# Background work of attention layer B split into steps that are issued a share apart, and weight scans reduced two loads later

## The chip, the cores and the metric

The kernel runs on one core of one Trainium2 chip. The metric is the time of one execution on the device in microseconds. One execution of each kernel is also profiled; its trace holds every instruction with start, duration and what released it.

The engines are called by the short names of the profile: PE is TensorE (matrix products and transposes; PEld is its weight load), DVE is VectorE, ACT is ScalarE, POOL is GpSimd, and SP is SyncE, which here issues the DMAs. SBUF is the on-chip memory that all engines read; PSUM is the memory into which PE writes its products.

## The reference

A two-layer encoder step over a prompt of 2048 rows and a sample of 64 rows, model width 1024. Each layer computes

```python
h = rms_norm(x, norm_g); q, k, v, gate = split(h @ w_in)
q, k = rms_norm per head(q) * q_g, rms_norm per head(k) * k_g     # heads of 64
s = q @ k.T * 64 ** -0.5 + bias          # bias depends on the distance only
p = softmax(s over a band of chunks of 64 rows)
x = x + ((p @ v) * silu(gate)) @ w_out
```

Layer A has 16 query heads on 2 key heads, a band of its own chunk and 2 before it, and a learned sink in the softmax. Layer B has 16 heads of its own for queries and keys, a band of its own chunk and 8 before it, and no sink. The sample attends to a cache of keys and values and to itself. Outputs are the two layers' result for prompt and sample and the newest keys and values of both layers.

## The kernel before

The program runs layer A, A's output projection, layer B, and B's output projection. The change bears on layer B. There the outer loop runs over 8 **head pairs** (two heads, 128 columns each of q, k, v and gate), the next one over **units** of 256 rows (8 of the prompt, then the sample), each of two **tiles** of 128 rows.

For each tile the input projection makes 512 columns in PSUM (`pj`, lines 673 to 680; the operands are split into high and low 16-bit parts, hence three products a step). `evacuate_b` copies q and k to `pa` (L714, ACT), the high part of v to `values` (L718, ACT), the low part of v (L719, DVE, which reads L718's result), and the gate to `pb` (L722, ACT). `head_norm` squares q and k (L755, POOL), sums per head (L756, DVE), adds epsilon and takes the power -1/2 (L759, L760, POOL), and scales q and k in place (L773, DVE). `gate` takes a tanh (L781, ACT) and multiplies (L782, DVE). PE transposes q and k (L843); ACT copies the high parts (L1357, L1358) and DVE subtracts for the low parts (L1369, L1373); small DMAs (L1362) copy query rows from one half of the partitions to the other.

The attention of a unit has four steps, one for each head and tile (`scores`): PE writes scores to one of **two** PSUM buffers named `sb` (L1418, L1419); DVE adds the bias and takes the row maximum (L1422, which writes `p` to SBUF and the maximum to `nm`, and so frees `sb`); DVE adds a constant to `nm` (L1427); ACT takes the exponential with its row sum (L1431); ACT and POOL split `p` in two 16-bit parts (L1465, L1466), which a transposing DMA turns (L1474). Some steps later PE multiplies with the values into the PSUM buffer `o` (L1563 and others; two halves for the high and the low part). After the fourth step DVE takes the inverse of the row sums (L1439), POOL multiplies it with the gate (L1450, tile `G`), PE transposes `G` into an `sb` buffer (L843), and ACT copies that to `gt` (L1237). `finish_pairs` adds the two halves of `o` (copy L1247 on ACT, sum L1249 on DVE, after which `o` is free), multiplies with `gt` (L1250, POOL), and the result is stored (L1252, SP). The sample has its own outputs (L1521, L1525 to L1528).

Layer B's weights are used in 16-bit parts, scaled by their largest entry. `scan` loads pieces of the next head pair's weights (and of the output weights and the cache) and DVE reduces each to its maximum (L174); `input_across`, `everywhere` make scales of them.

What sets the order: PE runs in the order in which the program is written. The other engines' instructions are put in order by the framework's scheduler, which simulates all engines; waits between engines are semaphores. Each engine then runs its list strictly in that order, so an instruction that waits holds up all that follow it. Evacuated tiles leave their remaining work in the queue `bg` (class `Background`): `put(cost, fn, urgent)` adds an item, and `share(least, parts, few)`, called after each attention step, runs items up to a cost of `max(1.8, cost / 4)`. What an item issues is tied behind the last softmax instruction of its engine (`anchor`). A `Filler` issues projection matmuls between the attention steps, so that PE has work, and `due` runs what an earlier step has left for a later one (`LAG = 4` steps for the turned products).

Of the kernel before, what the change touches and what calls it, by code (L numbers as in the profile page):

```python
# [34 lines left out]
WB = 3  # L35
# [15 lines left out]
LAG = 4  # L51
HALF = 5 * 2 * P
# [3 lines left out]
def hybrid_encoder_kernel(  # L56
# [114 lines left out]
    def scan(i=None):  # L171
        if pending:
            j, raw = pending.pop()
            nc.vector.tensor_reduce(  # L174
                most[:, j : j + 1], raw, axis=AX.X, op=ALU.max, apply_absolute_value=True
            )
# [15 lines left out]

    def across(a, b):
        ps = psum("tp", 512, 1)
# [14 lines left out]
    def everywhere(h, o):  # L209
        ps = psum("tp", 512, 1)  # L210
        nc.tensor.matmul(ps[:, 0:3], ones[0:1, 0:1].to_broadcast([1, P]), o, start=True, stop=True)
        nc.vector.tensor_copy(scl[:, h], ps[:, 0:3])
# [14 lines left out]
    def input_scales(h):  # L227
        everywhere(h, row[:, 20:23])
        nc.vector.tensor_scalar(gsb[:, h], gain[:, 1, :], S_W(h), 1.0, op0=ALU.mult, op1=ALU.mult)
# [25 lines left out]
    def scale_work(hp, u, e):  # L255
        at = 2 * u + e
        if hp < 7:
            if at < 8:
                scan(8 * (hp + 1) + at)
            elif at == 8:  # L260
                scan()
# [6 lines left out]
            if 11 <= at < 14 and i < 84:  # L268
                scan(i)
            elif at == 14:  # L270
                scan()
# [15 lines left out]
    def bias_vectors_a():  # L287
        oh = held["oh"]
        ps = psum("tp", 512, 1)
# [79 lines left out]
    class Background:  # L369
        def __init__(self):  # L370
            self.queue, self.anchors, self.cost, self.lazy = [], {}, 0.0, False

        def put(self, cost, fn, urgent=False, lazy=False, weights=False):
            it = Item()
            it.fn, it.cost, it.urgent, it.weights = fn, cost, urgent, weights
# [41 lines left out]
        def share(self, least, parts, few):  # L417
            left = sum(it.weights for it in self.queue)
            self.drain(max(least, self.cost / parts), 1 if left <= few else 2)

    bg = Background()

    def load_weights(g, *specs, scale=None):
        dt = F32R if scale is None else F16
# [80 lines left out]
    def load_act(  # L505
        src, o, T, squares=False, joint=False, lead=None, cache=None, cached=False, dt=F32R,
        rows=None, scale=None,
    ):
        x = Item()
# [123 lines left out]
    def token_rows(unit):  # L633
        _, T, tiles = unit
        ps = psum("tp", 512, 1)
# [75 lines left out]
    def evacuate_b(hp, tt, ps, g):  # L711
# [7 lines left out]
        nc.vector.scalar_tensor_tensor(  # L719
            vh[:, :, HD:P], v, c, vh[:, :, 0:HD], op0=ALU.mult, op1=ALU.subtract  # L720
        )
# [24 lines left out]
    def head_norm(n, src, spread=True):  # L746
# [3 lines left out]
        def squares():  # L750
            sq = t("sq", [P, 256], 2)
            f.append(t("f", [P, 4], 3))
            fv = f[0][:n, :H]
            if spread:
                nc.gpsimd.tensor_tensor(sq[:n, : H * HD], src, src, op=ALU.mult)  # L755
                nc.vector.tensor_reduce(  # L756
                    fv, sq[:n, : H * HD].rearrange("p (h d) -> p h d", d=HD), axis=AX.X, op=ALU.add
                )
                nc.gpsimd.tensor_tensor(fv, fv, small[:n, :H], op=ALU.add)  # L759
                nc.gpsimd.tensor_tensor(fv, fv, mhalf[:n, :H], op=ALU.pow)  # L760
# [8 lines left out]

        def scale():  # L770
# [4 lines left out]
        return [bg.put(0.15 * H, squares, True), bg.put(0.1 * H, scale, True)]  # L775

    def gate(n, g):
        def fn():
            W = g.shape[1]
            e = t("sq", [P, 256], 2)  # L780
            nc.scalar.activation(e[:n, :W], g, AF.Tanh, scale=0.5)  # L781
            nc.vector.scalar_tensor_tensor(g, e[:n, :W], 1.0, g, op0=ALU.add, op1=ALU.mult)  # L782

        return [bg.put(0.3, fn)]
# [6 lines left out]
    def store_kv(layer, rows, kn, v, kdst, vdst):  # L791
# [9 lines left out]
        return bg.put(0.1, fn)  # L801
# [64 lines left out]
    class Filler:  # L866
# [9 lines left out]
        def step(self):  # L876
            if self.gen is None:
# [22 lines left out]
            if not self.attending:  # L900
                bg.drain(FR * c)
# [9 lines left out]
    def layer_a():  # L911
# [4 lines left out]
        def add_unit(qd, place, unit):  # L916
# [59 lines left out]
            def first():  # L976
# [7 lines left out]
                for i, c in enumerate(both([project(it.tile, xc, st.w[qd], 512, o) for it, o in zip(mine, qgs)])):  # L984
                    if i == 7:
                        token_scales(unit, xc, psum("tp", 512, 1))
# [75 lines left out]
        def turned(it, done):  # L1062
            tp = psum("tp", 512, 1)
# [169 lines left out]
    def gate_t(GT, n, scale=0.5):  # L1233
        J = GT.shape[1]
# [7 lines left out]
    def finish_pairs(Ov, gtv, n, dst, later=False):  # L1242
# [5 lines left out]
        for hh, rows in enumerate(halves):  # L1248
            nc.vector.tensor_tensor(o1v[rows], Ov[0:64, :, hh, :], o1v[rows], op=ALU.add)  # L1249
        nc.gpsimd.tensor_tensor(o1v, gtv, o1v, op=ALU.mult)  # L1250
        if later:
            held["later"].append(lambda: store(dst, o1v))  # L1252
        else:
            store(dst, o1v)

    def layer_b():
# [4 lines left out]
        def add_unit(hp, unit):  # L1261
# [23 lines left out]
            def gen():  # L1285
# [9 lines left out]
                for e, (tt, t0, n) in enumerate(tiles):  # L1295
                    out = []
                    c = yield from project((tt, t0, n), xc, st.w[hp], 512, out)
                    if last:
# [3 lines left out]
                        it.todo += [sums] + head_norm(P, pr[:, 0:128]) + gate(P, it.gate[:, e, 0:HD])  # L1302
                        it.todo.append(
                            store_kv(1, slice(n, P), kn, v, kb_s[192:256, cols], vb_s[192:256, cols])
# [7 lines left out]
                    it.todo += head_norm(n, pr[:n, 0:256]) + gate(n, it.gate[:n, e])  # L1312
                    if it is its[0] and e == 0:
                        block_scales(TOK - OT)
                    if tt >= NT - 4:
                        o = (tt - (NT - 4)) * P
                        it.todo.append(
                            store_kv(1, slice(0, P), kn, v, kb_p[o : o + P, cols], vb_p[o : o + P, cols])
# [13 lines left out]
        def queries(it):  # L1332
# [8 lines left out]
            tp = psum("tp", 512, 1)  # L1341
# [43 lines left out]
        def scores(it, i, h):  # L1385
# [52 lines left out]
            if c == w - 1:  # L1438
                nc.vector.reciprocal(it.sm[:n, :w], it.sm[:n, :w])  # L1439
                if turned(it, 0) and len(TURNED) == 1:  # L1440
                    part = it.sm[:n, TURNED[0] : w : 2]
                    nc.vector.tensor_scalar(part, part, PB, 1.0, op0=ALU.mult, op1=ALU.mult)
                it.G = G = t("G", [P, 256])
                if u == NU:
                    nc.gpsimd.tensor_tensor(
                        G[:, 0:HD], it.gate[:, 0, 0:HD], it.sm[:, 0:1].to_broadcast([P, HD]), op=ALU.mult
                    )
                    return
                for e in range(len(tiles)):
                    nc.gpsimd.tensor_tensor(  # L1450
                        G[:n, e * P : (e + 1) * P].rearrange("p (h d) -> p h d", d=HD),
                        it.gate[:n, e].rearrange("p (h d) -> p h d", d=HD),
                        it.sm[:n, 2 * e : 2 * e + 2].unsqueeze(2).to_broadcast([n, 2, HD]),
                        op=ALU.mult,
                    )
# [60 lines left out]

        def sample_outputs(it):
            O = psum("o", 512, 1)
# [11 lines left out]
        def sample_turned(it):  # L1530
            tp = psum("o", 512, 1)
# [7 lines left out]
        def turned_products(it, h):  # L1539
# [3 lines left out]
            if h == 0:  # L1543
                it.O = psum("o", 512, 1)
# [26 lines left out]
        def gates(it):  # L1571
            u, T, tiles = it.unit
            n = tiles[0][2]
            GT = psum_b("sb", 1024, 2) if it.hp and len(TURNED) else psum("tp", 512, 1)
# [4 lines left out]
        def finish(it):  # L1579
# [6 lines left out]
                True,  # L1586
            )
            finished[1, u] = finished.get((1, u), 0) + 1

        def products(it, h):  # L1590
# [13 lines left out]
            def begin():  # L1604
                if h == 0:
                    it.O = psum("o", 512, 1)
# [23 lines left out]
        def pipeline():  # L1630
# [63 lines left out]
            while todo:  # L1694
                filler.to(filler.done + 2.6)
                due(step)
                step += 1
            flush()
# [228 lines left out]
```

## Time and profile before

| | |
|---|---|
| time, median of 3 runs (lowest to highest) | 2230.35 us (2230.12 to 2232.27) |
| the profiled execution's own time | 2230.04 us |
| its span in the profile | 2228.3 us |
| instructions | 40988 |
| mean granted clock of PE | 0.979 |
| busy: PE | 2078.6 us (93%) |
| busy: DVE | 1520.2 us (68%) |
| busy: ACT | 1436.8 us (64%) |
| busy: POOL | 1140.4 us (51%) |
| chain that ended last | PE 45%, DVE 21%, ACT 9%, DMA 9%, issue 8%, POOL 6% |
| layer A | about 0 to 650 us |
| A's output projection | to about 870 us |
| layer B | about 870 to 2050 us |
| B's output projection | to the end |

A row of a timeline gives start, duration, engine, line, operation, output and input by the program's names, shapes, and in brackets the engine's idle time before it with what released it. A row of the waits gives an engine's instruction, what it waited for, the time in total, how often, and the longest. Line numbers are those of the kernel before.

### The profile page before, as it was taken

The numbers are of one execution on the slowest core, as the hardware profiler recorded it, in microseconds if no ns is written. First come the engines' busy times: TensorE is split into PE (matmuls) and PEld (weight loads), VectorE is DVE, ScalarE is ACT, GpSimd is POOL, SyncE is SP. The second block draws the span as 40 slices with busy tenths as digits, with TensorE's granted clock in tenths as the row PEclk, the third lists the DMA queues.
The fourth block names the chain that finished last, engine by engine and source line by source line (L and its number), as shares of the span: only waits on it lengthen the run. The fifth ranks groups of instructions, "written<-read, shape, count | busy, mean of one in ns | idle before, by whom it ended". The sixth has DMA issues, their size and how long they took to land.

```text
span 2228.3 us, 40988 instructions
## 1 busy us (share of the span) xinstructions
PE 2078.6 (93%) x12951; PEld 1477.0 (66%) x12951; DVE 1520.2 (68%) x4049; ACT 1436.8 (64%) x3610; POOL 1140.4 (51%) x1621
## 2 busy tenths in 40 slices
PE   7999999999999999999988988899898898898999
PEld 6887888787889997555554544455455454456788
DVE  6769778677676456878676676766867767568542
ACT  6888778677784333666666666766766667567430
POOL 5645644343454456763565665656656566465100
PEclk9999999999999999999999999999999999999999
DMA  8856547756546667544677686886867858568764
GB/s 274 281 158 215 170 138 216 229 164 186 165 128 198 207 204 233 180 158 139 155 186 181 151 223 139 180 204 138 200 172 175 212 139 183 137 135 187 209 199 124
DMA packets 512122, 404.97 MB, mean 182 GB/s; under 512 B 303697, under 2 KB 449377, under 8 KB 511873
## 3 DMA queue, kind: packets, MB, share of 16 engines
q1 hardware_dynamic: 511904, 402.35, 66.3%
q8 instruction: 102, 1.67, 0.3%
q14 instruction: 116, 0.94, 0.1%
HBM read 257.59 MB, written 73.43 MB: 149 GB/s over the span
## 4 chain that ended last, share of the span: by engine, by line
PE 45%; DVE 21%; ACT 9%; DMA 9%; issue 8%; POOL 6%; SPq 1%; ACTq 0%; POOLq 0%; DVEq 0%
PE pj L678 7%; PE pj L680 7%; PE pj L679 7%; PE pj L1770 4%; PE pj L1772 4%; PE pj L1771 4%; DVE p L1422 4%; DVE pa L773 3%; DMA scan<-in_w_in_b_dram 3%; PE sa L843 2%; POOL values L1466 2%; DVE q L1369 2%; DVE o L1249 2%; ACT p L1431 2%; DMA scan<-in_w_o_b_dram 1%
## 5 line engine op out<-in xcount | busy, mean ns | idle before, releaser
L678 PE MATMUL pj<-wh,xx 128*128 128x512 f16 (+2 forms) x1648 | 649.1, 394 | 4.0 <-ACT pb L701 1.7
L680 PE MATMUL pj<-wh,xx 128*128 128x512 f16 (+2 forms) x1648 | 630.7, 383 | 2.4 <-POOL xx L563 2.4
L679 PE MATMUL pj<-wh,xx 128*128 128x512 f16 x1024 | 396.7, 387 | 0.9 <-DVE wh L469 0.9
L1431 ACT ACTIVATE p<-p,nm 128x640 f32<-128x640 f32 (+5 forms) x264 | 198.8, 753 | 250.6 <-DVE nm L1427 210.1
L1466 POOL TENSOR_TENSOR values<-p,values 128x640 f16<-128x640 f32 (+2 forms) x224 | 281.5, 1257 | 133.7 <-ACT values L1465 131.2
L1770 PE MATMUL pj<-xx,wh 128*128 128x264 f32 (+1 forms) x1024 | 291.2, 284 | 7.1 <-DVE res L1776 3.6
L1771 PE MATMUL pj<-xx,wh 128*128 128x264 f32 (+1 forms) x1024 | 288.6, 282 | 0.0
L679 PE MATMUL pj<-wl,xx 128*128 128x512 f32 (+1 forms) x624 | 234.3, 375 | 2.3 <-DVE wl L469 2.3
L563 POOL TENSOR_TENSOR xx<-xraw,xx 128x528 fp32r<-128x528 f32 (+4 forms) x144 | 184.0, 1296 | 88.9 <-ACT xx L562 82.4
L1422 DVE CUSTOM_DVE_ANT_0 p<-sb,BT 128x640 f32<-128x640 f32 (+5 forms) x272 | 195.9, 720 | 30.2 <-PE sb L1419 26.8
L760 POOL TENSOR_TENSOR f<-f,mhalf 128x4 f32<-128x4 f32 (+2 forms) x187 | 186.9, 999 | 13.4
L680 PEld LDWEIGHTS <-xx 128*128 128x128 f16 x1024 | 102.0, 100 | 130.3 <-issue 11.1
L1250 POOL TENSOR_TENSOR o<-gt,o 128x256 f32<-128x256 f32 (+1 forms) x132 | 102.4, 776 | 159.1 <-ACT p L1156 89.9
L773 DVE TENSOR_TENSOR pa<-pa,f 128x256 f32<-128x256 f32 (+3 forms) x221 | 150.4, 681 | 46.8 <-POOL f L760 42.2
L755 POOL TENSOR_TENSOR sq<-pa 128x256 f32<-128x256 f32 (+2 forms) x187 | 115.5, 618 | 107.6 <-ACT pa L714 66.3
L1156 ACT ACTIVATE p<-p,nm 128x257 f32<-128x257 f32 (+2 forms) x272 | 134.3, 497 | 48.7 <-DVE nm L1150 42.0
L678 PEld LDWEIGHTS <-xx 128*128 128x128 f16 x1024 | 102.2, 100 | 84.5 <-issue 6.3
L679 PEld LDWEIGHTS <-xx 128*128 128x128 f16 x1024 | 102.0, 100 | 83.8 <-issue 9.5
L1465 ACT CAST values<-p 128x640 f16<-128x640 f32 (+2 forms) x224 | 147.1, 657 | 5.8
L1772 PE MATMUL pj<-xx,wl 128*128 128x264 f32 x512 | 145.7, 285 | 0.3 <-DVE wl L462 0.3
L1772 PE MATMUL pj<-xx,wh 128*128 128x264 f16 x512 | 142.1, 277 | 0.0
L1150 DVE CUSTOM_DVE_ANT_0 p<-sa,BT,nsink 128x256 f32<-128x256 f32 (+2 forms) x272 | 117.4, 468 | 36.1 <-PE sa L843 31.4
(272 smaller groups left out, 5029.3 us busy)
## 6 DMA issues: line engine op xcount, KB each, us to landing
xx<-xsb SPq DMA_DIRECT2D x112, 512.0 KB, 4.2
xx<-xsa SPq DMA_DIRECT2D x88, 512.0 KB, 4.8
xraw<-oga SPq DMA_DIRECT2D x64, 264.0 KB, 3.5
xraw<-ogb SPq DMA_DIRECT2D x64, 264.0 KB, 3.9
xsa<-xx SPq DMA_DIRECT2D x32, 512.0 KB, 4.1
scan<-in_w_in_b_dram SPq DMA_DIRECT2D x64, 256.0 KB, 4.7
wl<-in_w_in_b_dram SPq DMA_DIRECT2D x64, 256.0 KB, 5.4
xraw<-in_x_dram SPq DMA_DIRECT2D x40, 256.0 KB, 4.0
```

Source lines behind the costliest of these rows:

```text
L563: nc.gpsimd.tensor_tensor(lo, rv, wide(hi), op=ALU.subtract)
L678: nc.tensor.matmul(ps[:n, :C], xh, wh, start=k == 0, stop=False)
L679: nc.tensor.matmul(ps[:n, :C], xh, wl, start=False, stop=False)
L680: nc.tensor.matmul(ps[:n, :C], xl, wh, start=False, stop=k == KC - 1)
L760: nc.gpsimd.tensor_tensor(fv, fv, mhalf[:n, :H], op=ALU.pow)
L773: nc.vector.tensor_tensor(sv, sv, fv.unsqueeze(2).to_broadcast([n, H, HD]), op=ALU.mult)
L1422: mi = nc.vector.tensor_tensor_reduce(out=p[r, :nk], in0=S[r, o : o + nk], in1=b, op0=ALU.add, op1=ALU.min, scale=1.0, scalar=3e38, accum_ ...
L1431: ex = nc.scalar.activation(p[:n, :nk], p[:n, :nk], AF.Exp, scale=-1.0, bias=it.nm[:n, c : c + 1], accum_out=it.sm[:n, c : c + 1],)
L1466: lo = nc.gpsimd.tensor_tensor(two[:, :, 1, :], pv, two[:, :, 0, :], op=ALU.subtract)
L1770: nc.tensor.matmul(ps[:, :OT], wh, oh, start=k == 0, stop=False)
L1771: nc.tensor.matmul(ps[:, :OT], wh, ol, start=False, stop=False)
L1772: nc.tensor.matmul(ps[:, :OT], wl, oh, start=False, stop=k == KC - 1)
```

## The change

Five things, all in the way that work is handed to `bg`.

- `evacuate_b`: the low part of v (L719) is an item of its own. `head_norm` in layer B (`apart=True`) becomes three items, squares, sums and scale, and `gate` two, tanh and product. An item can name one that must run before it (`after`), and `drain` skips it in the share in which that one ran (`tick`).
- `finish_pairs`: the sum L1249, the product L1250 and the store are an item that is put as urgent; the ACT copies L1247 are issued at once.
- `scores`: the inverse sums (L1439) and gate products (L1450) of a unit become an item, run at the latest by `gates`.
- `everywhere`: the copy of the scales (and the scaled gains) become an item.
- `scan`: a load is reduced when the next one but one has been issued (`keep=1`, three buffers `wraw` in place of two buffers `scan`).

Buffers: `sq` 4 in place of 2, `f` 4 in place of 3. Whatever reuses a PSUM buffer or needs a result runs the items that are left first (`run_all`, `tp_bank`, `o_bank`).

```diff
     def scan(i=None, keep=0):
-        if pending:
-            j, raw = pending.pop()
+        while len(pending) > keep:
+            j, raw = pending.pop(0)
...
-            raw = t("scan", [P, 512], 2)
+            raw = t("wraw", [P, 512], WB) if keep else t("scan", [P, 512], 1)
...
+    def run_all(name):
+        while held[name]:
+            bg.run(held[name].pop(0))
...
         def run(self, it):
+            if it.after is not None:
+                self.run(it.after)
+            it.tick = self.tick
...
         def drain(self, budget, most=KC):
+                if it.after is not None and (it.after.fn is not None or it.after.tick == self.tick):
+                    continue
...
-        nc.vector.scalar_tensor_tensor(
-            vh[:, :, HD:P], v, c, vh[:, :, 0:HD], op0=ALU.mult, op1=ALU.subtract
-        )
+        def low():
+            nc.vector.scalar_tensor_tensor(
+                vh[:, :, HD:P], v, c, vh[:, :, 0:HD], op0=ALU.mult, op1=ALU.subtract
+            )
+        held["rest"].append(bg.put(0.2, low, True))
...
-        return [bg.put(0.15 * H, squares, True), bg.put(0.1 * H, scale, True)]
+        first = bg.put(0.15 * H - 0.1 * apart, squares, True)
+        if not apart:
+            return [first, bg.put(0.1 * H, scale, True)]
+        second = bg.put(0.1 * H, sums, True, after=first)
+        return [first, second, bg.put(0.1 * H, scale, True, after=second)]
...
-        return [bg.put(0.3, fn)]
+        if not apart:
+            return [bg.put(0.3, curve)]
+        first = bg.put(0.2, curve)
+        return [first, bg.put(0.2, product, after=first)]
...
+        def fn():
+            for hh, rows in enumerate(halves):
+                nc.vector.tensor_tensor(o1v[rows], Ov[0:64, :, hh, :], o1v[rows], op=ALU.add)
+            nc.gpsimd.tensor_tensor(o1v, gtv, o1v, op=ALU.mult)
+            if key:
+                held["later"].append(last)
...
+        if key:
+            held["ends"].append(bg.put(0.8, fn, True))
...
             if c == w - 1:
-                nc.vector.reciprocal(it.sm[:n, :w], it.sm[:n, :w])
+                item = bg.put(0.8, fn, True)
+                if u != NU:
+                    it.inverse = item
...
+        def o_bank():
+            run_all("rest")
+            run_all("ends")
+            return psum("o", 512, 1)
```

Below is what the change makes of VectorE's list at three places of one head pair, before and after. In the rows, L1422 is the softmax (its second row reads out the row maximum), L1427 the addition to `nm`; the numbers behind the names tell the buffers apart. In the changed kernel the same instructions have other line numbers: L1422 is L1491, L1427 is L1496, L773 is L811, L782 is L831, L1439 is L1519, L719 is L749, L756 is L802, L1249 is L1306.

VectorE at the end of a unit, the norm scale of `pa_3538` and the unit's last softmax; before:

```order
L773 TENSOR_TENSOR pa_3538_18044<-pa_3538_18044,f_3545_18073 128x256
L1422 ISA p_3552_18108,nm_3527_17969<-sb_3551_18107,BT_95 128x640
L1422 ISA nm_3527_17969 128x1
L782 SCALAR_TENSOR_TENSOR pb_3514_17884<-sq_3550_18097,pb_3514_17884 128x128
L1427 TENSOR_SCALAR nm_3527_17969<-nm_3527_17969 128x1
L1439 RECIPROCAL sm_3526_17968<-sm_3526_17968 128x4
```

and changed:

```order
L1491 ISA p_3552_18106,nm_3527_17965<-sb_3551_18105,BT_95 128x640
L1491 ISA nm_3527_17965 128x1
L811 TENSOR_TENSOR pa_3538_18044<-pa_3538_18044,f_3545_18073 128x256
L831 SCALAR_TENSOR_TENSOR pb_3514_17882<-sq_3550_18096,pb_3514_17882 128x128
L1496 TENSOR_SCALAR nm_3527_17965<-nm_3527_17965 128x1
L1519 RECIPROCAL sm_3526_17964<-sm_3526_17964 128x4
```

The softmax stands ahead of the norm scale; the addition to `nm` and the inverse sums stay behind both.

VectorE in the next unit, around the second softmax (`p_3571` before, `p_3570` changed); before:

```order
L719 SCALAR_TENSOR_TENSOR values_2360_11645<-pj_3549_18086,values_2360_11645 128x2x64
L1427 TENSOR_SCALAR nm_3562_18172<-nm_3562_18172 128x1
L756 TENSOR_REDUCE f_3566_18185<-sq_3565_18184 128x4
L1422 ISA p_3571_18211,nm_3562_18172<-sb_3570_18210,BT_95 128x640
L1422 ISA nm_3562_18172 128x1
L773 TENSOR_TENSOR pa_3558_18159<-pa_3558_18159,f_3566_18185 128x256
L782 SCALAR_TENSOR_TENSOR pb_3548_18085<-sq_3567_18191,pb_3548_18085 128x128
L1427 TENSOR_SCALAR nm_3562_18172<-nm_3562_18172 128x1
L1422 ISA p_3577_18256,nm_3562_18172<-sb_3576_18255,BT_95 128x640
```

and changed:

```order
L749 SCALAR_TENSOR_TENSOR values_2360_11645<-pj_3549_18084,values_2360_11645 128x2x64
L1496 TENSOR_SCALAR nm_3562_18165<-nm_3562_18165 128x1
L802 TENSOR_REDUCE f_3566_18182<-sq_3565_18181 128x4
L225 TENSOR_SCALAR gsb_91<-gain_77,scl_90 128x8
L1491 ISA p_3570_18205,nm_3562_18165<-sb_3569_18204,BT_95 128x640
L1491 ISA nm_3562_18165 128x1
L1496 TENSOR_SCALAR nm_3562_18165<-nm_3562_18165 128x1
L811 TENSOR_TENSOR pa_3558_18156<-pa_3558_18156,f_3566_18182 128x256
L831 SCALAR_TENSOR_TENSOR pb_3548_18083<-sq_3567_18186,pb_3548_18083 128x128
```

The addition to `nm` that belongs to this softmax has moved from behind the norm scale and the gate product to directly behind the softmax.

VectorE where that unit ends, around the sum of `o` (`o1_3600` before, `o1_3599` changed); before:

```order
L1439 RECIPROCAL sm_3561_18171<-sm_3561_18171 128x4
L782 SCALAR_TENSOR_TENSOR pb_3548_18085<-sq_3582_18293,pb_3548_18085 128x128
L1249 TENSOR_TENSOR o1_3600_18363<-o_3572_18227,o1_3600_18363 64x256 x2
L773 TENSOR_TENSOR pa_3578_18276<-pa_3578_18276,f_3581_18287 128x256
L1422 ISA p_3605_18378,nm_3603_18376<-sb_3604_18377,BT_95 128x640
L1422 ISA nm_3603_18376 128x1
L469 SCALAR_TENSOR_TENSOR wh_3594_18330<-wl_3586_18303,gsb_91,wh_3594_18330 128x512
L1427 TENSOR_SCALAR nm_3603_18376<-nm_3603_18376 128x1
```

and changed:

```order
L831 SCALAR_TENSOR_TENSOR pb_3548_18083<-sq_3582_18288,pb_3548_18083 128x128
L1519 RECIPROCAL sm_3561_18164<-sm_3561_18164 128x4
L811 TENSOR_TENSOR pa_3578_18273<-pa_3578_18273,f_3581_18286 128x256
L1491 ISA p_3604_18370,nm_3602_18368<-sb_3603_18369,BT_95 128x640
L1491 ISA nm_3602_18368 128x1
L1306 TENSOR_TENSOR o1_3599_18358<-o_3572_18224,o1_3599_18358 64x256 x2
L496 SCALAR_TENSOR_TENSOR wh_3593_18326<-wl_3585_18295,gsb_91,wh_3593_18326 128x512
L1496 TENSOR_SCALAR nm_3602_18368<-nm_3602_18368 128x1
```

The sum of the two halves of `o` has moved from ahead of the norm scale and the next unit's first softmax to behind both.

PE's list is the same in both kernels, instruction by instruction, and so are all lists up to the end of layer A's output projection. ACT's L722 no longer carries a wait for DVE and stands directly behind L718.

More of the change, by code (lines that the diff above doesn't have):

```diff
@@ L51 @@
 LAG = 4
+SQB = 4
 HALF = 5 * 2 * P
@@ L421, in hybrid_encoder_kernel @@
     bg = Background()
+    held["rest"], held["ends"], held["scales"] = [], [], []
     def load_weights(g, *specs, scale=None):
+        run_all("scales")
         dt = F32R if scale is None else F16
@@ L1247, in finish_pairs, with fn, last @@
             nc.scalar.copy(o1v[rows], Ov[64:128, :, hh, :])
[L1248 to L1252, printed above, removed]
+        def fn():
+            for hh, rows in enumerate(halves):
[3 more added lines that the diff above has]
+                held["later"].append(last)
+            else:
+                store(dst, o1v)
+        def last():
+            store(dst, o1v)
+            finished[key] = finished.get(key, 0) + 1
+        if key:
+            held["ends"].append(bg.put(0.8, fn, True))
         else:
-            store(dst, o1v)
+            fn()
     def layer_b():
@@ L1697, in pipeline @@
                 step += 1
+            run_all("ends")
             flush()
```

147 lines of the change are left out of this document (91 added, 56 removed).

## The prediction

> **What bounds the kernel now.** I read the stages first (the windows view; after the stretch and its length come the busy time of PE, PEld, DVE, ACT and POOL with their instructions, PE's granted clock, the DMA share and GB/s), because the diff touches only what surrounds layer B.
>
> ```profile
> 870.00:2050.00 1180.00, 1065.50 (x6229) 609.38 (x6230) 835.34 (x2165) 790.19 (x1957) 706.96 (x948) 0.97 0.70 172
> ```
>
> PE is the bound: it works 1065.5 of layer B's 1180 us, and no other engine passes 71%. What can be had is PE's idle 114.5 us and a little clock. The work is the same before and after, and PE's own order is the same instruction by instruction, so the time changes only by how long PE stands. Next came what PE waited for in this stretch (engine and line, what it waited for, us in total, times, longest).
>
> ```profile
> PE sb L1418 <- DVE nm L1422: 46.9, 26, 3.9
> PE sb L1418 <- DMA q<-q: 12.7, 5, 4.3
> ...
> PE sb L843 <- DVE nm L1422: 5.4, 5, 1.7
> PE sb L1418 <- ACT gt L1237: 4.2, 7, 0.7
> ```
>
> The scores (L1418) have two PSUM buffers, and the softmax on VectorE (L1422) frees them: 46.9 us are PE waiting for VectorE to get to it. The same waits list over all engines tells why VectorE is late: it runs its list in order, and often the head of that list is itself waiting.
>
> ```profile
> ACT pb L722 <- DVE values L719: 64.1, 66, 2.4
> ...
> DVE o L1249 <- ACT o L1247: 39.3, 42, 1.4
> DVE pa L773 <- POOL f L760: 37.4, 40, 2.0
> ...
> DVE most L174 <- DMA scan<-in_w_in_b_dram: 30.2, 15, 4.6
> ```
>
> Last came PE's timeline. Layer B repeats per head pair; the gaps of one repetition are these (start, us, line, then in brackets the idle time before it and its releaser; two rows without a bracket are used further down).
>
> ```profile
> 1389.66 0.32 PE L1418 MATMUL sb<-KA,q 128*128 128x384 f16 x1 [2.24 <-DVE nm L1422]
> ...
> 1392.97 0.32 PE L1418 MATMUL sb<-KA,q 128*128 128x384 f16 x1
> ...
> 1407.18 0.32 PE L1418 MATMUL sb<-KA,q 128*128 128x384 f16 x1 [1.49 <-DVE nm L1422]
> ...
> 1410.49 0.32 PE L1418 MATMUL sb<-KA,q 128*128 128x384 f16 x1 [0.66 <-ACT gt L1237]
> ...
> 1422.60 0.32 PE L1418 MATMUL sb<-KA,q 128*128 128x384 f16 x1 [1.64 <-DVE nm L1422]
> ...
> 1427.78 1.26 PE L1563 MATMUL o<-pt,values 128*128 128x256 f16 x12
> ...
> 1437.92 0.41 PE L843 MATMUL sb<-ident,G 128*128 128x128 f32 x2 [0.94 <-DVE nm L1422]
> ...
> 1441.64 0.32 PE L1418 MATMUL sb<-KA,q 128*128 128x384 f16 x1 [2.66 <-DVE nm L1422]
> ...
> 1468.31 0.32 PE L1418 MATMUL sb<-KA,q 128*128 128x384 f16 x1 [2.25 <-DMA q<-q]
> ...
> 1486.24 0.36 PE L1521 MATMUL o<-VS,ph 128*128 128x256 f32 x1 [1.06 <-ACT p L1431]
> ```
>
> I call them A (1389.66), B (1407.18), C (1410.49), D (1422.60), E (1437.92), F (1441.64), Q (1468.31) and S (1486.24). Four of them, A, B, D and F, are L1418 waiting for L1422, and that wait occurs 26 times: 26 / 4 = 6.5 repetitions. So I price one repetition and multiply by 6.5.
>
> **Part by part.**
>
> *Norm scale behind the softmax (A, B, C).* In the changed order L1422 stands ahead of the norm scale L773. Here are the rows around A, with a second L773 for comparison.
>
> ```profile
> 1387.13 1.61 DVE L773 TENSOR_TENSOR pa<-pa,f 128x256 f32<-128x256 f32 x1
> 1388.77 0.82 DVE L1422 CUSTOM_DVE_ANT_0 p<-sb,BT 128x640 f32<-128x640 f32 x1
> ...
> 1389.72 0.15 DVE L1427 TENSOR_SCALAR nm<-nm 128x1 f32<-128x1 f32 x1
> ```
>
> ```profile
> 1387.07 1.39 POOL L1466 TENSOR_TENSOR values<-p,values 128x640 f16<-128x640 f32 x1 [0.55 <-ACT values L1465]
> ```
>
> ```profile
> 1426.03 0.43 DVE L773 TENSOR_TENSOR pa<-pa,f 128x256 f32<-128x256 f32 x1
> ```
>
> ```profile
> 1392.44 0.47 ACT L1237 ACTIVATE gt<-sb,scl 128x256 f32<-128x256 f32 x1
> ```
>
> Swapped, L1422 starts at 1387.13 instead of 1388.77, so A's direct part is 1.6 of 2.24, and B, with the same swap, loses all its 1.49. But A is followed by a score at 1392.97 that starts just as the gate copy L1237 ends (1392.44 + 0.47 = 1392.91): that hangs on the last exponential, which waits for L1427, and L1427 still stands behind both. So PE, early at A, stands at the gate copy instead; after B the same happens at C, which grows. What stays is by how much the pair gets shorter. L773 takes 1.61 where it starts beside L1466 on POOL and 0.43 otherwise; it ends at 1388.74, 0.28 after L1466 (1387.07 + 1.39 = 1388.46). Begun 0.82 later, it would still end at about 1388.75, with L1422 already done: L1427 0.77 earlier. Bounds for A, B and C together: 0 if L773 always takes 1.61, and 2.24 + 1.49 = 3.73 if C does not grow. I take 2 x 0.77 = **-1.5**, the value of the rows next to it. [...] By a fixed 1.61 this term would be 0.
>
> *Softmax log sum ahead of norm and gate (D).*
>
> ```profile
> 1414.85 1.40 DVE L782 SCALAR_TENSOR_TENSOR pb<-sq,pb 128x128 f32<-128x128 f32 x1
> 1416.17 0.14 DVE L1427 TENSOR_SCALAR nm<-nm 128x1 f32<-128x1 f32 x1
> ```
>
> ```profile
> 1416.40 0.83 ACT L1431 ACTIVATE p<-p,nm 128x640 f32<-128x640 f32 x1 [1.59 <-DVE nm L1427]
> ```
>
> ```profile
> 1419.70 0.48 DVE L1369 SCALAR_TENSOR_TENSOR q<-tp,qf,q 64x256 f16<-64x256 f32 x1 [2.46 <-ACT KB L1358]
> ```
>
> D's chain backwards: L1422 stood behind L1369 and L1373, these waited 2.46 us for ScalarE's K copy, ScalarE's exponential before that copy had waited 1.59 for L1427, and L1427 stood behind L773 and a gate product that took 1.40. In the changed order this L1427 stands directly behind its softmax, ahead of both. The exponential then starts when ScalarE is free, 1.59 earlier, and everything behind it too: **-1.6** of D's 1.64. Bounds 0 and -1.64.
>
> *V's low part later, with ScalarE's L722 no longer behind it.* The 64.1 us of ScalarE's waits for L719 go, but off the path: what ScalarE hands to PE there waits for L1427 anyway. Only where L719 stood straight ahead of L1422 is something gained, at F.
>
> ```profile
> 1435.38 0.69 DVE L174 TENSOR_REDUCE most<-scan 128x1 f32<-128x512 f32 x1 [1.56 <-DMA scan<-in_w_in_b_dram]
> ...
> 1440.56 0.29 DVE L719 SCALAR_TENSOR_TENSOR values<-pj,values 128x128 f16<-128x128 f32 x1
> ```
>
> F: **-0.3** (the 0.29 of L719). Bounds 0 and -0.3: the rest of F's wait is L1369 and L1373, which do not move.
>
> *Scans two loads late (E).* In the changed order the reductions L174 and their loads stand where they stood, relative to the softmaxes and to SP's transfers, at nearly every place, only under another buffer's name. So E, whose L1422 stands behind the 1.56 us wait of L174, stays: 0. Worse, that landing is set by the DMA and not by PE; what PE gained since A (1.5 + 1.6) meets it. Bounds 0 (the load is issued earlier by as much) and +3.1 (it lands at the old time); nothing in the trace decides, and I take the middle, **+1.5**.
>
> *O sum later (Q, S, and the bank).* L1249 now stands behind the next softmax.
>
> ```profile
> 1464.43 0.56 ACT L1431 ACTIVATE p<-p,nm 128x320 f32<-128x320 f32 x1 [0.80 <-DVE nm L1422]
> ```
>
> Q: the query copy follows this exponential, which waited 0.80 for a sample softmax behind L1249. That softmax now stands ahead: **-0.8** of Q's 2.25; bounds 0 and -2.25.
>
> ```profile
> 1425.15 0.85 DVE L1249 TENSOR_TENSOR o<-o,o 64x256 f32<-64x256 f32 x2 [0.48 <-ACT o L1247]
> ...
> 1426.37 0.82 DVE L1422 CUSTOM_DVE_ANT_0 p<-sb,BT 128x640 f32<-128x640 f32 x1
> ```
>
> ```profile
> L1249 DVE TENSOR_TENSOR o<-o,o 64x256 f32<-64x256 f32 x124 | 51.6, 416 | 40.9 <-ACT o L1247 39.3 <-PE pj L680 0.6
> ```
>
> The price is the O bank: L1249 ended at 1426.00, and PE fills the bank again at 1427.78, so it had 1.78 us to spare; behind L773 and L1422 it ends 0.43 + 0.82 = 1.25 later. That leaves 0.5, hence 0 here. At S the shift reaches PE: L1521 gets some 1.2 us later, and its next gap, for POOL, shrinks by as much, so direct cost 0; bounds 0 and +1.2.
>
> *The other edits.* The inverse sums L1439 keep their place, so POOL's wait for them stays. The sum of squares L756 and the gate product L782 go a few places back, out of the way of L1422, and PE needs neither at once: 0. SP, which also issues in order, has the store of the O block (now L1254) behind one or two more transposes, and what stands behind it there, the query copies and loads, moves by a place.
>
> ```profile
> SPq L1252 <- POOL o L1250: 85.7, 35, 8.2
> ```
>
> That store waits 85.7 us for POOL, 2.4 a time, and the only thing of SP's that PE waits for is the query copy (12.7 us). Bounds -12.7 to +12.7 in all; I take 0, since the store's feeder and the store move by like amounts.
>
> *The clock.*
>
> ```profile
> 1380.00:1390.00 10.00, 7.66 (x45) 4.08 (x44) 7.91 (x17) 5.61 (x15) 5.36 (x6) 1.00 0.80 184
> 1440.00:1450.00 10.00, 8.36 (x41) 4.27 (x41) 9.91 (x25) 8.84 (x20) 8.06 (x10) 0.83 1.12 206
> 1470.00:1480.00 10.00, 10.00 (x54) 5.93 (x53) 3.70 (x12) 5.67 (x15) 5.50 (x7) 0.83 0.95 318
> ```
>
> After F (2.66) and Q (2.25) the granted clock was 0.83, about 10 x 0.17 = 1.7 us lost each; around A (2.24) it was 1.00. So the edge lies near 2.2 us here. Q falls to 1.45 and F stays above. I take -1.0 for Q (1.7, not certain) and +0.4 for S, which grows to 2.3 (1.7 at one chance in four): **-0.6**; bounds -1.7 and +1.7. [...]
>
> *Sum.* -1.5 - 1.6 - 0.3 + 1.5 - 0.8 - 0.6 = -3.3 us a repetition, times 6.5 = -21.5. The profiled execution took 2230.04, the median is 2230.35; in the median's frame 2230.35 - 21.5 = 2208.9, said as 2209. Layer A's order is untouched: 0.
>
> **The rivals.**
>
> *Slower: the O bank (0.21).* Mechanism: PE, no longer held at A to D, reaches the next O product before L1249 has freed its bank. It decides where L1249 ends more than 1.78 us later against PE than now; 1.25 are used up by the order alone, and any wait ahead of it (L773 for POOL, 37.4 us in 40 cases, is up to 2.0 long) takes the rest. There are 124 / 2 = 62 such units; 0.5 us lost at each is +31, and 1.7 of clock at S, 6.5 times, +11; of the gains (1.5 + 1.6 + 0.3 + 0.8 + 1.0 = 5.2 a repetition, 34 in all) two thirds stay, -23, +19 in all: 2249. Milder, with 0.3 us a unit, +7: 2237. Against it: at no unit of the trace does PE now wait for L1249 for long.
>
> *No change (0.09).* C, E and S give all back, since PE only walks to the next thing with a fixed time: 2228 to 2233.
>
> *Much faster (0.12).* The waits for L1422 go in full (46.9 + 5.4 = 52.3) and C and E do not grow: 2178. Against it: the rows at 1392.97.
>
> [...]
>
> **How the numbers follow.** Forecast 0.50, much faster 0.12, clock not won 0.08: faster 0.70. No change 0.09; slower 0.21. A difference under 0.2% (4.5 us) can't be told from none by a measurement of this kernel. The range reaches down to 2182, nearly the much faster case (without E's +1.5 the sum is -4.8 x 6.5 = -31, 2199, well inside), and up to 2238, the milder O bank; outside are about 1 in 10 on each side.
>
> **What would show it.** Right: L1418's waits for L1422 in layer B fall from 46.9 to under 30; D gone; waits for the gate copy L1237 (4.2 now) up by several us; ScalarE's waits for L719 near 0; L174's waits for the DMA about the same. Wrong: PE's waits for L1249 or for POOL ahead of L1563 and L1521 over 15 us in sum (the O bank), 0.83 clock windows more often than before, or layer B's stretch as long as now.

## The result, and the profile after

The changed kernel takes 2199.05 us (median of 4 runs, 2192.94 to 2200.77) against 2230.36 for the kernel before: a ratio of 0.9853, 95% interval 0.9833 to 0.9873. It is faster by 1.5%, 31 us; the forecast was 2209, 21 us. The line numbers in the rows that follow are those of the kernel they come from; the map stands with the change (L1422 is L1491, L1249 is L1306, L773 is L811), and further L1418 is L1487, L1369 is L1438, L1521 is L1606, L174 is L175.

The stage of layer B in the windows view ends some 30 us earlier, here the stretch from 870 to 2020:

```profile
870.00:2020.00 1150.00, 1066.97 (x6273) 613.79 (x6272) 822.78 (x2180) 784.24 (x1962) 715.98 (x950) 0.97 0.73 178
```

PE works as long as before (1066.97 against 1065.50) and stands for 83.0 us in place of 114.5 us. What it waited for in layer B (us in total, times, longest):

```profile
PE sb L1487 <- DMA q<-q: 14.5, 11, 2.6
PE sb L1487 <- DVE nm L1491: 12.8, 8, 2.5
PE o L1606 <- DVE o L1306: 12.3, 7, 2.3
...
PE sb L1487 <- ACT gt L1292: 3.5, 5, 1.2
...
PE sb L895 <- DVE nm L1491: 2.6, 4, 0.8
```

The waits for the softmax fell from 46.9 + 5.4 to 12.8 + 2.6 us. In their place stands a wait that was 1.6 us before, the sample's products for the sum of `o` (12.3), and the query copies are the largest wait now. VectorE's own waits fit the cause:

```profile
DVE p L1491 <- PE sb L1488: 60.2, 43, 7.3
...
DVE most L175 <- DMA wraw<-in_w_in_b_dram: 34.5, 24, 3.2
DVE pa L811 <- POOL f L806: 27.5, 46, 1.5
```

The softmax on VectorE now waits 60.2 us for PE's scores, where it waited 24.1 before: VectorE is more often there when they come. Its wait for ScalarE's copy of `o` fell from 39.3 to 2.4 us, and ScalarE's wait for the low part of v (64.1) is gone; the scan loads of `in_w_in_b` and `in_w_o_b` are waited for 54.4 us (34.5 + 19.9) against 47.7 (30.2 + 17.5). In PE's timeline, the repetition of which the prediction showed the gaps:

```profile
1386.14 0.32 PE L1487 MATMUL sb<-KA,q 128*128 128x384 f16 x1 [0.30 <-DMA q<-q]
...
1403.76 0.32 PE L1487 MATMUL sb<-KA,q 128*128 128x384 f16 x1 [1.76 <-DMA q<-q]
...
1435.10 0.32 PE L1487 MATMUL sb<-KA,q 128*128 128x384 f16 x1 [1.74 <-DVE nm L1491]
...
1461.28 0.32 PE L1487 MATMUL sb<-KA,q 128*128 128x384 f16 x1 [2.20 <-DMA q<-q]
...
1479.98 0.55 PE L1606 MATMUL o<-VS,ph 128*128 128x256 f32 x1 [2.20 <-DVE o L1306]
```

They are A, B, F, Q and S. A fell from 2.24 to 0.30; C, D and E have no row; at B another wait, for the query copy, is now the last; S grew from 1.06 to 2.20. This repetition is not typical at E and F: in three of the six others E is still 0.51 to 0.77 (0.94 before) and F is 2.46 or 2.47 (2.66 before).

**Counted over all head pairs.** PE's order is the same in every kernel here, so one can lay the traces side by side score tile by score tile (33 a head pair) and take the time from one tile's start to the next. Means over the last seven head pairs, in us, one profile a kernel; the columns hold the intervals around the gaps, the last one a whole head pair:

| kernel | A | B, C | D | E, F | Q | S | head pair |
|---|---|---|---|---|---|---|---|
| before | 10.02 | 9.22 | 6.44 | 12.13 | 24.85 | 9.74 | 145.37 |
| changed | 7.89 | 9.04 | 4.78 | 10.66 | 24.70 | 9.49 | 139.63 |
| norm alone | 8.28 | 8.69 | 5.82 | 11.46 | 24.34 | 9.09 | 140.76 |
| sum of `o` alone | 10.10 | 9.25 | 4.67 | 12.02 | 22.23 | 10.51 | 142.43 |
| low part of v alone | 8.72 | 10.13 | 6.08 | 12.41 | 22.86 | 9.25 | 142.72 |
| changed, unit 6 at once | 7.97 | 8.80 | 4.34 | 10.96 | 24.61 | 8.44 | 138.10 |

Seven pairs at -5.74 are -40.2 us, more than the 29.3 by which the profiled span fell. The rest went elsewhere, mostly ahead of layer B: its first score tile starts at 900.83 in place of 893.75 (below). The profile of the norm alone is the fastest of its six runs (2199.46 us, where their median is 2208.58), so its row may be too low.

### The profile page after: what moved, and what is told of

Read it like the earlier page. It is cut to its first block, busy times and chain, and to the rows that moved or that the text cites. A ratio compares the mean times of both kernels' runs of the same rounds, so it can differ in the third digit from the quotient of the medians.

```text
span 2199.0 us, 40839 instructions
## 1 busy us (share of the span) xinstructions
PE 2074.1 (94%) x12951; PEld 1476.7 (67%) x12951; DVE 1503.6 (68%) x4049; ACT 1428.2 (65%) x3610; POOL 1149.4 (52%) x1621
## 4 chain that ended last, share of the span: by engine, by line
PE 52%; DVE 15%; DMA 12%; ACT 8%; POOL 6%; issue 5%; SPq 2%; ACTq 0%; POOLq 0%; DVEq 0%
PE pj L706 8%; PE pj L708 8%; PE pj L707 8%; PE pj L1856 5%; PE pj L1858 5%; PE pj L1857 5%; DMA wraw<-in_w_in_b_dram 4%; DVE p L1491 2%; PE sa L895 2%; POOL values L1546 2%; PE o L1648 2%; DVE pa L811 2%; DMA xraw<-in_x_rows_dram 2%; PE tp L895 2%; DMA wraw<-in_w_o_b_dram 1%
## 5 line engine op out<-in xcount | busy, mean ns | idle before, releaser
L1491 DVE CUSTOM_DVE_ANT_0 p<-sb,BT 128x640 f32<-128x640 f32 (+5 forms) x272 | 195.5, 719 | 64.8 <-PE sb L1488 61.4
L806 POOL TENSOR_TENSOR f<-f,mhalf 128x4 f32<-128x4 f32 (+2 forms) x187 | 191.4, 1024 | 12.9
L811 DVE TENSOR_TENSOR pa<-pa,f 128x256 f32<-128x256 f32 (+3 forms) x221 | 143.3, 648 | 37.1 <-POOL f L806 32.4
```

The costliest lines, as they stand in the source:

```text
L811: nc.vector.tensor_tensor(sv, sv, fv.unsqueeze(2).to_broadcast([n, H, HD]), op=ALU.mult)
L1491: mi = nc.vector.tensor_tensor_reduce(out=p[r, :nk], in0=S[r, o : o + nk], in1=b, op0=ALU.add, op1=ALU.min, scale=1.0, scalar=3e38, accum_ ...
```

## The experiments

**One part alone.** Three kernels take over one part each. In the second the sum of `o` is deferred, for example, and everything else, but for the larger buffers, runs as before:

```diff
         if key:
             held["ends"].append(bg.put(0.8, fn, True))
...
-        held["rest"].append(bg.put(0.2, low, True))
+        low()
-        norm = head_norm(n, pr[:n, 0:256], apart=True)
+        norm = head_norm(n, pr[:n, 0:256])
```

The norm alone:

> The kernel before with one part of the change: the norm in layer B in three items (squares, sums, scale). In VectorE's order the norm scale stands behind the softmax at 58 places, as in the changed kernel; the sum of o and the low part of v stay where they were. By the terms of the prediction: A, B and C together -1.5 us a repetition, and the addition to nm at D now ahead of the norm scale but still behind the gate product, so at most half of D (0 to -0.8); times 6.5 that is -10 to -15, 2215 to 2220 us. Rival 'one swap does it all' (the softmax waits vanish once the norm scale is out of the way): 2200 to 2205. Rival 'handed back at the gate copy': 2228 to 2232.

2208.58 us, ratio 0.9886 (0.9866 to 0.9906): -24, beyond the -10 to -15 and short of the rival's 2200 to 2205. The sum of `o` alone:

> The kernel before with one part of the change: the sum of the two halves of o and what follows it (finish_pairs) as an item of its own. VectorE's sum of o stands behind the next softmax at 69 places. At D the addition to nm stands directly behind its softmax. By the terms of the prediction: D -1.6, Q -0.8, clock -0.6, together -3.0 a repetition, times 6.5 -20, so about 2211 us. Rival 'the O bank' (the bank comes free later than PE needs it): 0.3 to 0.5 us at 62 units, +19 to +31 before the gains, so 2229 to 2241; its waits of PE for the sum of o in layer B would be over 15 us, where the full change has 12.3.

2222.72 us, 0.9954 (0.9936 to 0.9971): -10, half of the forecast. By the table it won 2.9 a head pair, as priced in sum (-3.0): D -1.8 and Q -2.6, with S +0.8. Its time does not show that, since its layer B starts late as well (900.38) and its first head pair took 2.6 longer. The low part of v alone:

> The kernel before with one part of the change: the low part of v as an item of its own, behind the softmax at 37 places, and ScalarE's gate copy without its wait for VectorE. By the term of the prediction (F alone, -0.3 a repetition, times 6.5) -2 us, 2228 us. Rival: the 64.1 us that ScalarE waited for it were on the path after all, and a good part of them is gained: 2215 or less.

2216.11 us, 0.9926 (0.991 to 0.9942): -16 where I had -2, near the size of the rival (2215 or less), though not for its reason, as shown next. PE's waits in the three (norm; sum of `o`; low part):

```profile
PE sb L1483 <- DVE nm L1487: 24.4, 14, 3.6
PE sb L1483 <- DMA q<-q: 12.6, 9, 2.7
PE o L1601 <- DVE o L1302: 9.6, 6, 2.5
```

```profile
PE sb L1483 <- DVE nm L1487: 44.7, 24, 5.0
PE o L1601 <- DVE o L1302: 17.8, 6, 3.5
...
PE sb L1483 <- DMA q<-q: 4.6, 3, 2.4
```

```profile
PE sb L1483 <- DVE nm L1487: 49.0, 25, 5.0
PE o L1601 <- DVE o L1302: 10.4, 6, 2.0
...
PE sb L1483 <- DMA q<-q: 5.5, 3, 3.3
```

The norm part halves the waits for the softmax (46.9 to 24.4). The other two leave them and more than halve the waits for the query copies (12.7 to 4.6 and 5.5). Where the low part gains this stands ahead of the sample. ScalarE there, in the kernel before and in the one with the low part alone:

```profile
1453.59 0.27 ACT L718 ACTIVATE values<-pj 128x128 f16<-128x128 f32 x1
1456.37 0.83 ACT L1431 ACTIVATE p<-p,nm 128x640 f32<-128x640 f32 x1 [2.51 <-DVE nm L1427]
...
1457.20 0.35 ACT L722 ACTIVATE pb<-pj,scl 128x128 f32<-128x128 f32 x1
```

```profile
1452.62 0.27 ACT L742 ACTIVATE values<-pj 128x128 f16<-128x128 f32 x1
1452.77 0.37 ACT L750 ACTIVATE pb<-pj,scl 128x128 f32<-128x128 f32 x1
1453.02 0.84 ACT L1496 ACTIVATE p<-p,nm 128x640 f32<-128x640 f32 x1
```

The exponential (L1431, L1496) starts 0.40 after the v copy's start, not 2.78. The gate copy did not hold it: before, L722 stands behind the exponential and waits for nothing here. The exponential waited 2.51 us for VectorE's addition to `nm`. VectorE at this place, in the same two kernels (L773 and L807 are the norm scale, L1422 and L1487 the softmax, L1427 and L1492 the addition):

```profile
1452.64 1.61 DVE L773 TENSOR_TENSOR pa<-pa,f 128x256 f32<-128x256 f32 x1 [1.18 <-POOL f L760]
1454.18 0.81 DVE L1422 CUSTOM_DVE_ANT_0 p<-sb,BT 128x640 f32<-128x640 f32 x1
...
1456.12 0.15 DVE L1427 TENSOR_SCALAR nm<-nm 128x1 f32<-128x1 f32 x1
```

```profile
1450.59 0.83 DVE L1487 CUSTOM_DVE_ANT_0 p<-sb,BT 128x640 f32<-128x640 f32 x1 [1.08 <-PE sb L1484]
...
1451.34 0.42 DVE L807 TENSOR_TENSOR pa<-pa,f 128x256 f32<-128x256 f32 x1
...
1452.27 0.15 DVE L1492 TENSOR_SCALAR nm<-nm 128x1 f32<-128x1 f32 x1
```

With the low part alone, too, the softmax stands ahead of the norm scale here. Counted over the traces, of 221 norm scales 12 stand behind more softmaxes than before with the low part alone, and 12 with the sum of `o` alone, ten of them the same; with the norm alone it is 64, in the changed kernel 70. So the three parts make in part one and the same move. That may be why their gains do not add up; no run undoes that move by itself. What follows the exponential is early as well: the first copy of the queries on ScalarE starts 4.3 us behind the sample's scores (1461.52 and 1457.25) and not 6.8 (1464.99 and 1458.20), and Q's gap is not there.

**One part less.** The changed kernel with one part undone:

> The changed kernel with the norm in two items again, as before; all other parts of the change stay. Alone, this part gained 23.7 us (2208.6 against 2232.3), the sum of o 9.6 and the low part of v 16.2, 49.5 together, where the full change gains 31 to 33. Theory 'the norm carries it': without it the other two keep at most their 25.8 and meet the same waits of the scores for the softmax, 2207 to 2223 us. Rival 'the parts remove the same waits, whichever is there': under 2204.

2204.56 us, 0.9884 (0.9864 to 0.9905). This lies between the two expectations. The other two parts keep -26.6, the sum of what they gained alone (25.8), and PE's scores wait 31.2 us for the softmax, where it is 12.8 in the full change.

> The changed kernel with the sum of o issued at once, as before; all other parts of the change stay. Theory 'the O bank costs': PE's 12.3 us of waits for the sum of o in the changed kernel go, or most of them, and the norm and the low part of v keep up to their 39.9 (23.7 + 16.2), so 2190 to 2196 us. Rival 'the parts add up, short by a fixed share': this part's 9.6 are lost, 2205 to 2209.

2192.31 us, 0.9826 (0.9809 to 0.9842): inside the first theory's range. Norm and low part add up (-38.9 against 39.9).

> The changed kernel with the low part of v issued at once, as before; all other parts of the change stay. Theory 'ScalarE's order is a gain of its own' (alone it was 16.2 us, where the prediction had 2): 2208 to 2216 us, and PE waits more for the query copies than the 14.5 us of the changed kernel. Rival 'the softmax order is what counts, and the norm part has it already': 2197 to 2202.

2192.62 us, 0.9834 (0.9813 to 0.9854): neither. Undoing this part costs nothing. So any two parts are worth their sum or more, and the third on top brings little or nothing. The intervals of the last two overlap that of the full change, so that the full change is slower than these is likely by the medians but not settled by them. The gate in two items and the later inverse sums are in all three of these kernels and in none of the kernels with one part alone; what they are worth was not tested apart.

> The changed kernel with the item of the sum of o put at the head of the queue rather than behind the other urgent items; it still stands behind the next softmax. Theory 'the O bank': the bank comes free up to 0.43 us earlier (one norm scale) and PE's waits for the sum of o fall from 12.3 us toward 9, so 2194 to 2199 us. Rival: the order of the queue is made anew by the scheduler and nothing moves, 2197 to 2202.

2196.19 us, 0.9842 (0.9825 to 0.9859). PE's waits for the sum of `o` went from 12.3 to 11.1 us, within what profiles differ: inconclusive.

> The changed kernel with the scans reduced one load late, as before. VectorE's order relative to the softmaxes is that of the changed kernel at every place. Theory 'the scans do nothing': the time of the changed kernel, 2193 to 2201 us. Rival 'the later reduction saves waits for the load': 2205 us or more, with more of VectorE's waits for scan loads than the 54.4 us (34.5 + 19.9) of the changed kernel.

2201.94 us, 0.9859 (0.984 to 0.9877), by the ratio the changed kernel: no effect of the scans shows, as their unmoved order said.

**The O bank at the sample.** The last four ran side by side. The edit:

```diff
-        if key:
+        if key and key[1] not in (NU - 2,):
             held["ends"].append(bg.put(0.8, fn, True))
```

> The changed kernel itself, once more, so that the three others stand beside it on the same chip. Every theory: 2193 to 2201 us, a ratio to the kernel before of 0.983 to 0.987.

2199.94 us, 0.9858 (0.9845 to 0.9872).

> The changed kernel, but the sum of o of unit 6, the last before the sample, is issued at once, as before, so that the bank is free when the sample's products need it; the other units keep their later sum. Theory 'the O bank costs at the sample': the two intervals in which PE waits for L1306 ahead of L1606 took 9.49 us a head pair in the changed kernel and 8.43 with no later sum at all, so -1.06 times 8: 2190 to 2192 us, and PE's 12.3 us of waits for L1306 all but gone. Rival 'handed back at the next wait': 2196 to 2201, with those waits gone but the softmax waits up by as much.

2189.58 us, 0.9812 (0.9799 to 0.9826), below the interval of the full change beside it: -10.4. PE's waits for the sum of `o` ahead of the sample's products fell from 12.7 to 4.0 us; those for the softmax, 11.1 in the full change beside it, are 12.9:

```profile
PE sb L1487 <- DMA q<-q: 15.8, 13, 2.2
PE sb L1487 <- DVE nm L1491: 12.9, 7, 2.5
```

So the late sum of unit 6 costs the change 10 us. Only a part of that is standing: PE's idle time in layer B is 85.0 us (from 870 to 2010) against 88.6 in the full change beside it (870 to 2020). The other part is the clock. In windows of ten us, the clock below 1.00 costs layer B 28.9 us in the full change beside it and 20.5 with unit 6 at once. In both traces of the full change it fell behind three of the five S gaps of over 2 us, by some 1.7 us each (ten us at 0.83), so about 5 of these 8.4 us, an estimate, belong to S; the rest are falls elsewhere. In the changed kernel the ten microseconds behind the S gap of 2.20, and the same place with unit 6 at once (S at 0.57):

```profile
1480.00:1490.00 10.00, 10.00 (x52) 5.82 (x53) 3.83 (x17) 5.56 (x19) 6.35 (x11) 0.83 0.53 126
```

```profile
1480.00:1490.00 10.00, 10.00 (x63) 5.74 (x61) 6.04 (x20) 6.34 (x20) 4.56 (x9) 1.00 0.55 142
```

PE is busy all of the time in both, with 52 instructions at 0.83 and 63 at 1.00.

> As the last, with the sum of o of units 5 and 6 both issued at once. Theory: besides -1.06 at the sample's products, the four score intervals behind the sample, 24.59 us a head pair in the changed kernel and 23.48 with no later sum, fall too: -2.2 times 8, 2181 to 2185 us, the fastest version. Rival 'the later sum of unit 5 is what lets the sample's softmax go ahead at Q, and losing it costs what unit 6 gains': 2190 to 2199.

2189.17 us, 0.9811 (0.9798 to 0.9825): neither. Unit 5 brings nothing more, and it does not cost what unit 6 gained.

> As the last, and the low part of v issued at once, as before. Without it the changed kernel took 2192.6 us (this and the full change differ by 6). Theory 'the low part's place costs nothing once the norm is out of the way': 2180 to 2188 us. Rival 'it is needed where the sum of o is early, as the two together gained 38.8 with the norm': 2192 to 2200.

2187.44 us, 0.9798 (0.9781 to 0.9815), as the theory had it. It is the fastest median, but its interval overlaps those of the two before it. These three beat both the kernel before and the full change by their intervals; the simplest of them is the exception for unit 6 alone.

## Why the prediction was right, step by step

**Right.** The bound (PE, and how long it stands) and the mechanism (the head of VectorE's list waits, and the softmax behind it holds the score buffers) are shown: the waits for L1422 fell by 36.9 of 52.3 us. Of the 34.1 us at the scores, the norm part alone takes 22.5; with it undone the waits there stand at 31.2 us again, with the sum of `o` undone at 25.0, with the low part of v undone at 17.5, in the full change at 12.8.

The total came nearer than its parts. The forecast was -3.3 us a repetition, 6.5 times; measured are -5.74 in each of seven head pairs, -40. Some 11 us outside of them, which the forecast had at 0, bring this back to the -29 of the profiles. That -21 and -31 lie so close is in part luck.

*A, B, C*: forecast -1.5 a repetition, measured -2.3 (10.02 + 9.22 to 7.89 + 9.04). The pair of norm scale and softmax got shorter as priced. Around B in the changed kernel, VectorE and then POOL:

```profile
1401.33 0.82 DVE L1491 CUSTOM_DVE_ANT_0 p<-sb,BT 128x640 f32<-128x640 f32 x1
...
1402.08 0.86 DVE L811 TENSOR_TENSOR pa<-pa,f 128x256 f32<-128x256 f32 x1
```

```profile
1401.27 1.40 POOL L1546 TENSOR_TENSOR values<-p,values 128x640 f16<-128x640 f32 x1 [0.54 <-ACT values L1545]
```

The norm scale took 0.86 in place of 1.61 and ended 0.27 after the POOL row (1402.94 and 1402.67), as the forecast had it (0.28). The trace of the kernel before shows it all over layer B: the 43 norm scales of 128x256 that start while L1466 runs on POOL end 0.27 to 0.29 us after it and so take from 0.43 to 1.62, by how much of it is left; of the 64 that start with POOL idle 63 take 0.39 to 0.43. What was wrong is where the gain would be handed back: not at the gate copy behind A (A's part stays, and the waits for the gate copy went from 4.2 to 3.5 us, not up) but at B itself, where the query copy is late next.

*D*: forecast -1.6, measured -1.66; in five of the seven head pairs the gap of 1.64 is gone. The step in between shows it: the queries' low parts wait 0.16 for ScalarE's K copy and no longer 2.46.

```profile
1413.87 0.48 DVE L1438 SCALAR_TENSOR_TENSOR q<-tp,qf,q 64x256 f16<-64x256 f32 x1 [0.16 <-ACT KB L1427]
```

*Scans*: nothing, as forecast.

*S*: forecast 0 direct and +0.4 of clock, measured -0.25 (9.74 to 9.49). The gap grew to 2.20 (forecast 2.3), and the next one, in which PE waited for POOL (9.1 us in 6 waits before), is no longer there. What the forecast did not weigh is a version without the later sum at this one place: against that the full change costs 1.3 a repetition (10.4 / 8; in the table 1.05 in column S). To that extent the rival's mechanism, the O bank that comes free too late, was real, at the sample alone: the other units' products wait for L1306 once, for 0.3 us.

*The clock*: forecast -0.6. In windows of ten us its loss in layer B went from 37.4 to 32.3 us, -0.7 a head pair. The 0.08 that the forecast gives to a clock not won is the author's estimate: no run shows a clock term of 0, and in its place stand the 5.1 us between these two.

**Mis-sized.** *E and F*: forecast +1.2 (E +1.5, F -0.3), measured -1.5. Of the 10.2 us that the seven head pairs gained there, the fourth (the one shown) and the seventh make 8.9; in three others E shrank a little and F by 0.2, about as priced. E's charge did not come. It was the middle between a load that follows PE and one that lands at its old time; the 1.56 us wait of L174 at E is again 1.56 in the changed kernel (at 1429.06, 6.3 us earlier), so the load follows, and the charge should have been at its lower end, 0. Why the two head pairs gained more was not taken apart.

*Low part of v*: forecast -0.3 a repetition, -2 in all; alone it measured -16. That ScalarE waits for L1427 anyway held: ahead of the sample its wait was for L1427. The step that failed is that the part would gain only where L719 stood straight ahead of L1422. The scheduler makes VectorE's whole list anew, and in it the softmax moved ahead of the norm scale at 12 places. In the full change the other two parts had taken the same time.

*Q*: forecast -0.8 and -1.0 of clock, measured -0.15 in the table. The gap stayed at 2.20 in the repetition shown. The mean hides two things: in the seventh head pair, where PE waits for `KB` and not for a query copy, the interval grew by 2.8; in the other six it fell by 0.6 in the mean, near the -0.8. Still, each of sum and low part alone takes 2.0 to 2.6 from this column and any two parts 1.5 to 2.2 (23.38, 23.28 and 22.60 without norm, sum and low part), all three together do not: here the third part costs what it gains elsewhere. Why is not settled.

*The inverse sums*: forecast that POOL's wait for them stays. It fell from 104.2 to 58.2 us (L1450, now L1530, waiting for L1439, now L1519); whether PE gains by it was not tested.

*Ahead of layer B*: forecast 0. In the thirteen profiles of kernels with the changed buffers the first score tile of layer B starts at 894.6 to 903.2 us, in the one profile of the kernel before at 893.75; in the changed kernel 4.7 of its 7.1 arise between 15 and 102 us. The order of the lists there is the same. What the thirteen share are the buffers (`sq` 4, `f` 4), and a kernel with those alone was not tried: whether this is the change or the spread of one profile stays open. It makes 7.1 of the 11 us between the -40 of the table and the -29 of the profiles.

## What to carry to other kernels

On an engine that runs its list strictly in order, look not for the slow instruction but for the one that waits at the head with a buffer's release behind it; put what frees a buffer of the bound engine ahead of it (here PE's waits for the softmax fell from 52.3 to 15.4 us). Where a scheduler makes the list, compare the whole list after each edit: an edit in one place moved the softmax in others. Several such edits may remove the same waits: their single gains (50 us here) are no forecast of the whole (31), and leaving one out is worth a run. A release that is put off must be checked against every user of that buffer; here one of nine units a head pair, the one before the sample, cost a third of the gain.

## What was not expected of the hardware

In the changed kernel a gap of 2.20 us at S was followed by ten microseconds at a granted clock of 0.83, and one of 2.29 (at 1341.55, the head pair before) by ten at 1.00:

```profile
1341.55 0.36 PE L1606 MATMUL o<-VS,ph 128*128 128x256 f32 x1 [2.29 <-DVE o L1306]
```

```profile
1340.00:1350.00 10.00, 8.45 (x52) 5.03 (x53) 5.55 (x22) 5.47 (x19) 6.17 (x11) 1.00 0.59 104
```

One of 2.64 (at 1181.27) was followed by 1.00 as well. The kernel before has the same: 0.83 behind a gap of 2.23 (at 1243.89) and 1.00 behind the 2.24 of A. So the edge near 2.2 us that the forecast read is none: from 2.2 to 2.6 us the length of the gap alone does not decide here whether the clock falls.

Runs of one kernel differ in the clock as well as in the time: the norm alone ran in 2199.46 us at a mean granted clock of 0.988 and in 2211.78 at 0.980. The clock does not settle the time: another run took 2206.94 at 0.980.
